# Three instead of two of eight gate and up tiles with seven products, and four low parts per block by a negative copy and an accumulating DMA

## The chip, the cores and the metric

The kernel runs on one core of a Trainium2 chip. The time is device microseconds of one launch. The engines are named as the profile names them: PE is TensorE (PEld its weight loads), ACT ScalarE, DVE Vector, POOL GpSimd, SP the engine that issues most DMAs.

## What is computed

One layer of an encoder trunk on 256 rows of 2048 float32 numbers: an input projection, three mixers, an output projection, then a SwiGLU block and a last norm. There is one layer; `w_gate` and `w_up` are 2048 by 5632. The change is in the two products `h @ w_gate` and `h @ w_up`.

```python
def rmsnorm(x, g):
    xf = x.astype(jnp.float32)
    y = xf * lax.rsqrt(jnp.mean(xf * xf, axis=-1, keepdims=True) + NORM_EPS)
    return (y * g.astype(jnp.float32)).astype(x.dtype)

def reference(x, positions, attn_norm_g, w_in, hg_lower_bounds, hg_norm_g, sb_norm_g,
              mla_q_norm_g, mla_w_uq, mla_kv_norm_g, mla_w_ukv, mla_out_norm_g, w_o,
              ffn_norm_g, w_gate, w_up, w_down, final_norm_g):
    ...
    for layer in range(DEPTH):
        h = rmsnorm(x, attn_norm_g[layer])
        hq, hf, hi, hg, sq, sk, sv, c_q, c_kv_rope = jnp.split(h @ w_in[layer], split_at, axis=-1)
        ...
        x = x + jnp.concatenate([hg_out, sb_out, mla_out], axis=-1) @ w_o[layer]
        h = rmsnorm(x, ffn_norm_g[layer])
        x = x + (jax.nn.silu(h @ w_gate[layer]) * (h @ w_up[layer])) @ w_down[layer]
    return rmsnorm(x, final_norm_g)
```

## The kernel before

**Matmuls in two halves.** A float32 operand is split into a high part in float32r and a low part, the rest: `hi = copy(raw)` on ScalarE, `lo = raw - hi` on Vector (L93, called by `split_w` at L107 and `halve` at L866). A product is then three matmuls: activation high times hi, activation high times lo, activation low times hi.

**The gate and up stage** (the loop over `g`, L933) has eleven blocks of 512 columns. In each, the inner dimension of 2048 is cut into eight tiles of 256. A plain tile loads one slab of w_gate and one of w_up, 512 KB each, as `raw` (L860), splits both, and `plain_unit` (L906) does 24 matmuls of 512 columns: two row halves (b) by gate and up by two inner halves (j) by three. They add into four accumulators c11, c21 (gate) and c12, c22 (up).

**The first two tiles (`FAST = 2`) are done with seven products instead of eight** (Strassen's scheme in Winograd's form, on a 2 by 2 grid of inner half by gate/up). `fast_weights` (L873) loads the up slab and the gate slab into one tile `W`, Vector makes four combinations `T`, and all operands are split (`hT`, `lT` for the combinations, `hi`, `lo` for those that are used as they are). The activations' eight forms are made once, in `turn_x2` (L812). The products fall into two groups: ACROSS (p1, p6, p7, p5) go into four PSUM banks and are shared by several outputs; ALONE (c11, c21, c12) go straight into accumulators. A fast tile has 7 x 3 = 21 matmuls. The loop first does ACROSS for all fast tiles, then ALONE for all, then sums the banks into u1 to u4 on Vector, then runs the plain tiles. At the block's end the accumulators are added, Silu is applied on ScalarE, and the result is turned by transposes in later blocks (`turn_hid`, L919, one step per plain tile by `tick`).

**Buffers.** raw, hi and lo have four slots each, `W`, `T`, `hT` and `lT` two each. A slot is written again when its last reader is done. The order on each engine is fixed when the program is built: a scheduler sorts by priority, and the loads and splits of weights stand 400 places ahead (`tc.high_priority(offset=ahead[0])`), so those of the next block are mixed into this one. Every engine's queue runs in order: an instruction that waits holds those behind it. SP issues the loads, in order too.

Of the kernel before, what the change touches and what calls it, by code (L numbers as in the profile page):

```python
# [9 lines left out]
F32 = mybir.dt.float32  # L10
F32R = mybir.dt.float32r
# [44 lines left out]
FAST = 2  # L56
# [4 lines left out]
def build(tc, x, xT, pos, gains, fgain, lbraw, w_in, w_uq, w_ukv, w_o, w_gate, w_up, w_down, cst, msk, out, dbg=None):  # L61
# [740 lines left out]
    def wo_end(a, g):  # L802
# [9 lines left out]
        def turn_x2():  # L812
            yield
            for i in range(2):
# [9 lines left out]
                A = ffp.tile([P, 8, P], F32, name=nm("T"), tag="T")  # L824
# [47 lines left out]

    def fast_weights(wa, wb, r0, c0):  # L873

        with tc.high_priority(offset=ahead[0]):
            W = ffp.tile([P, 4, 512], F32, name=nm("W"), tag="W")
            for w, js in ((wb, slice(0, 2)), (wa, slice(2, 4))):
                at = ROWS[w.tensor.name] * c0 + r0 * 512
                sp.dma_start(W[:, js, :], w[at:at + 2 * P * 512].rearrange("(p t c) -> p t c", p=P, t=2))
            T = ffp.tile([P, 4, 512], F32, name=nm("T"), tag="T")  # L880
            tt(T[:, 0:2, :], W[:, 0:1, :].broadcast_to([P, 2, 512]), W[:, 1:3, :], ALU.subtract)
            tt(T[:, 2, :], W[:, 1, :], T[:, 1, :], ALU.subtract)
            tt(T[:, 3, :], W[:, 3, :], T[:, 2, :], ALU.subtract)
            hT = ffp.tile([P, 4, 512], F32R, name=nm("hT"), tag="hT")
            lT = ffp.tile([P, 4, 512], F32R, name=nm("lT"), tag="lT")
            a = halve(W[:, 2:4, :], slice(0, 2))
            halve(T, slice(0, 2), hT, lT)
            halve(T, slice(2, 4), hT, lT)
            b = halve(W[:, 0:2, :], slice(1, 2))
        return a, b, (hT, lT)  # L890


    ACROSS = (("p1", 0, 0, 0), ("p6", 5, 2, 2), ("p7", 6, 2, 0), ("p5", 4, 2, 1))
    ALONE = (("c11", 2, 0, 1), ("c21", 3, 2, 3), ("c12", 7, 1, 1))

    def fast_unit(accs, products, ws, forms, start):
        ah, al = forms
        for name, f, which, k in products:
            hi, lo = ws[which]
            o = accs[name]  # L900
            last = name[0] == "p" and start == "last"
            pe.matmul(o, lhsT=ah[:, f, :], rhs=hi[:, k, :], start=start is True, stop=False)  # L902
            pe.matmul(o, lhsT=ah[:, f, :], rhs=lo[:, k, :], start=False, stop=False)  # L903
            pe.matmul(o, lhsT=al[:, f, :], rhs=hi[:, k, :], start=False, stop=last)  # L904
# [200 lines left out]
```

## Time and profile before

| | us |
|---|---|
| three runs | 1128.09, 1128.75, 1130.96 |
| median | 1128.75 |
| the profiled execution | 1129.1 |
| its span, first to last instruction | 1127.4 |
| one block of the gate and up stage in it | 43.3 |

The page gives busy time by engine and a mean over the whole run; stages differ, so the gate and up stage (about 400 to 877 us of the span) is read by itself, from the table of stretches and the timelines. A matmul's record is longer than its share of time, since matmuls overlap: the distance from start to start counts. The same holds, by less, for ScalarE and Vector.

### The profile page before, as it was taken

How to read it: one execution, taken by the hardware profiler on the slowest of the kernel's cores; microseconds unless marked ns; L12 is line 12 of the kernel's file. 1: busy time of each engine (PE TensorE's matmuls, PEld its weight loads, DVE VectorE, ACT ScalarE, POOL GpSimd, SP SyncE). 2: the span in 40 equal slices, each digit the busy share in tenths (PEclk: the TensorE clock that was granted, in tenths of full speed). 3: DMA queues.
4: the chain of work that ended last, by engine and by line, in shares of the span. 5: the costliest groups of instructions: out<-in, count | busy, mean ns of one | idle time of the engine just before them, and what ended most of it. 6: DMA issues, size and time to landing. Idle time of an engine off the chain costs nothing.

```text
span 1127.4 us, 14328 instructions
## 1 busy us (share of the span) xinstructions
PE 1112.2 (99%) x5363; PEld 942.3 (84%) x5363; DVE 758.9 (67%) x907; ACT 595.6 (53%) x793; POOL 77.4 (7%) x112
## 2 busy tenths in 40 slices
PE   8999999999999999999999999999999999999997
PEld 4888899999988888888888888888888888888886
DVE  7798555556557786786886887876967645454543
ACT  7664566566546654553554554554546534343433
POOL 3197000011100000000000000000000000000000
PEclk9999999999999999999999999999999999999999
DMA  7745455544776665655655656656638665666662
GB/s 259 245 152 164 123 170 179 168 134 157 217 250 203 218 214 187 204 191 189 201 191 184 207 185 204 197 171 209 198 119 291 205 197 188 194 195 189 189 198 99
DMA packets 73302, 215.18 MB, mean 191 GB/s; under 512 B 7440, under 2 KB 24592, under 8 KB 73232
## 3 DMA queue, kind: packets, MB, share of 16 engines
q1 hardware_dynamic: 72656, 212.16, 58.9%
q10 hardware_dynamic: 576, 2.10, 0.5%
q8 instruction: 42, 0.69, 0.2%
q14 instruction: 28, 0.23, 0.1%
HBM read 210.04 MB, written 4.19 MB: 190 GB/s over the span
## 4 chain that ended last, share of the span: by engine, by line
PE 95%; issue 1%; DVE 1%; ACT 1%; DMA 1%; POOL 0%; SPq 0%; ACTq 0%; POOLq 0%; DVEq 0%
PE acc L154 15%; PE acc L155 15%; PE acc L153 15%; PE acc L913 11%; PE acc L914 11%; PE acc L912 11%; PE bank L248 2%; PE bank L902 2%; PE bank L903 2%; PE bank L904 2%; PE acc L902 1%; PE acc L903 1%; PE acc L904 1%; DVE lo L93 1%; PE bank L411 1%
## 5 line engine op out<-in xcount | busy, mean ns | idle before, releaser
L93 DVE TENSOR_TENSOR lo<-raw,hi 128x1024 fp32r<-128x1024 f32 (+3 forms) x366 | 424.5, 1168 | 276.5 <-ACT hi L121 215.6
L121 ACT CAST hi<-raw 128x1024 fp32r<-128x1024 f32 (+3 forms) x234 | 223.1, 957 | 243.6 <-PE acc L155 220.7
L153 PE MATMUL acc<-hi,at 128*128 128x512 f32 (+2 forms) x808 | 304.8, 379 | 0.8 <-ACT hi L121 0.8
L154 PE MATMUL acc<-lo,at 128*128 128x512 f32 (+2 forms) x808 | 302.5, 375 | 3.0 <-DVE lo L93 2.8
L155 PE MATMUL acc<-hi,at 128*128 128x512 f32 (+2 forms) x808 | 301.4, 373 | 0.0
L912 PE MATMUL acc<-hi,at 128*128 128x512 f32 x528 | 207.5, 393 | 0.0
L914 PE MATMUL acc<-hi,at 128*128 128x512 f32 x528 | 205.8, 390 | 0.0
L913 PE MATMUL acc<-lo,at 128*128 128x512 f32 x528 | 205.7, 390 | 0.0
L869 ACT CAST hi<-raw 128x1024 fp32r<-128x1024 f32 x132 | 136.7, 1052 | 129.9 <-PE acc L914 95.8
L154 PEld LDWEIGHTS acc<-lo,at 128*128 128x128 f32 x808 | 152.1, 188 | 29.0 <-DVE lo L93 7.2
L153 PEld LDWEIGHTS acc<-hi,at 128*128 128x128 f32 x808 | 151.9, 188 | 23.9 <-ACT hi L121 1.9
L155 PEld LDWEIGHTS acc<-hi,at 128*128 128x128 f32 x808 | 151.9, 188 | 21.9
L913 PEld LDWEIGHTS acc<-lo,at 128*128 128x128 f32 x528 | 99.2, 188 | 20.6 <-DVE lo L93 0.7
L914 PEld LDWEIGHTS acc<-hi,at 128*128 128x128 f32 x528 | 99.1, 188 | 20.7
L912 PEld LDWEIGHTS acc<-hi,at 128*128 128x128 f32 x528 | 99.2, 188 | 19.8
L177 POOL TENSOR_TENSOR sm<-sm,expo 128x4 f32<-128x4 f32 (+2 forms) x14 | 12.0, 857 | 895.7 <-DVE sm L102 895.7
L93 DVE TENSOR_TENSOR lo<-W,hi 128x1024 fp32r<-128x1024 f32 (+1 forms) x44 | 42.0, 957 | 34.6 <-ACT hi L869 34.6
L869 ACT CAST hi<-W 128x1024 fp32r<-128x1024 f32 (+1 forms) x44 | 36.7, 834 | 49.8 <-PE acc L914 42.7
L93 DVE TENSOR_TENSOR lT<-T,hT 128x1024 fp32r<-128x1024 f32 x44 | 52.7, 1218 | 0.0
L869 ACT CAST hT<-T 128x1024 fp32r<-128x1024 f32 x44 | 45.2, 1049 | 0.3 <-DVE T L93 0.2
L93 DVE TENSOR_TENSOR T<-W,T 128x512 f32<-128x512 f32 x44 | 30.1, 684 | 0.1
L93 DVE TENSOR_TENSOR T<-W 128x1024 f32<-128x1024 f32 x22 | 26.9, 1221 | 1.4 <-DMA W<-w_gate 1.1
(254 smaller groups left out, 1097.4 us busy)
## 6 DMA issues: line engine op xcount, KB each, us to landing
raw<-w_down SPq DMA_DIRECT2D x88, 512.0 KB, 3.5
raw<-w_gate SPq DMA_DIRECT2D x66, 512.0 KB, 4.1
raw<-w_up SPq DMA_DIRECT2D x66, 512.0 KB, 4.4
raw<-w_in SPq DMA_DIRECT2D x48, 384.0 KB, 3.6
raw<-w_in SPq DMA_DIRECT2D x32, 512.0 KB, 3.6
raw<-w_o SPq DMA_DIRECT2D x32, 512.0 KB, 3.9
W<-w_up SPq DMA_DIRECT2D x22, 512.0 KB, 3.7
W<-w_gate SPq DMA_DIRECT2D x22, 512.0 KB, 4.6
```

The costliest lines, as they stand in the source:

```text
L93: dve.tensor_tensor(o, a, b, op=op)
L121: act.copy(hi[:, js, :n], raw[:, js, :n])
L153: pe.matmul(o, lhsT=ah, rhs=hi[:, j, cs], start=start and j == 0, stop=False)
L154: pe.matmul(o, lhsT=ah, rhs=lo[:, j, cs], start=False, stop=False)
L155: pe.matmul(o, lhsT=al, rhs=hi[:, j, cs], start=False, stop=stop and j == 1)
L869: act.copy(hi[:, js, :], src[:, js, :])
L902: pe.matmul(o, lhsT=ah[:, f, :], rhs=hi[:, k, :], start=start is True, stop=False)
L903: pe.matmul(o, lhsT=ah[:, f, :], rhs=lo[:, k, :], start=False, stop=False)
L904: pe.matmul(o, lhsT=al[:, f, :], rhs=hi[:, k, :], start=False, stop=last)
L912: pe.matmul(o, lhsT=ah, rhs=hi[:, j, :], start=start and nme == "c22" and j == 0, stop=False)
L913: pe.matmul(o, lhsT=ah, rhs=lo[:, j, :], start=False, stop=False)
L914: pe.matmul(o, lhsT=al, rhs=hi[:, j, :], start=False, stop=stop and j == 1)
```

## The change

`FAST` becomes 3, so each block has three fast and five plain tiles. In tiles 4 to 7 (`BYDMA`) the low part of the up slab is no longer subtracted on Vector: ScalarE writes `hi = copy(raw)` and then `lo = -hi`, and a DMA issued from POOL adds `raw` to `lo` in place (`halve_by_dma`). The four combinations are laid out anew: three in `T`, the fourth overwrites the first quarter of `W` (the up slab's first half, which is not needed any more); the gate slab comes as two DMAs of 256 KB. `hT`/`lT` hold what ACROSS needs (three combinations and one slab half as it is), and `alone_weights` splits what ALONE needs later. The products run as ACROSS of tiles 0 and 1, ALONE of 0, ACROSS of 2, ALONE of 1, ALONE of 2. `W` has three slots now, `T` one; the activations' forms (`A`) and four of the later stage's tiles move to other tags.

```diff
--- before.py
+++ after.py
@@ -53,7 +53,8 @@
 SABBUFS = 3
 WARM = 9
 RAWS = 4
-FAST = 2
+FAST = 3
+BYDMA = (4, 5, 6, 7)
 MAGIC = 12582912.0
 LOGEXP = "natural_log_exp_and_others"
 
@@ -821,7 +822,7 @@
                     x2T[n] = at
                     continue
 
-                A = ffp.tile([P, 8, P], F32, name=nm("T"), tag="T")
+                A = ffp.tile([P, 8, P], F32, name=nm("T"), tag="T", bufs=1)
                 for j in range(2):
                     act.activation(A[:, 2 * j:2 * j + 2, :], ps[:, j * 256:(j + 1) * 256].rearrange("p (b n) -> p b n", b=2),
                                    AF.Copy, scale=gc(G_FFN, 2 * n + j))
@@ -870,38 +871,54 @@
         tt(lo[:, js, :], src[:, js, :], hi[:, js, :].bitcast(F32), ALU.subtract)
         return hi, lo
 
+    def halve_by_dma(src):
+
+        hi = slabp.tile([P, 2, 512], F32R, name=nm("hi"), tag="hi")
+        lo = slabp.tile([P, 2, 512], F32R, name=nm("lo"), tag="lo")
+        act.copy(hi, src)
+        act.activation(lo, hi.bitcast(F32), AF.Copy, scale=-1.0)
+        pool.dma_start(lo, src, accum_op=ALU.add)
+        return hi, lo
+
     def fast_weights(wa, wb, r0, c0):
 
         with tc.high_priority(offset=ahead[0]):
-            W = ffp.tile([P, 4, 512], F32, name=nm("W"), tag="W")
-            for w, js in ((wb, slice(0, 2)), (wa, slice(2, 4))):
-                at = ROWS[w.tensor.name] * c0 + r0 * 512
-                sp.dma_start(W[:, js, :], w[at:at + 2 * P * 512].rearrange("(p t c) -> p t c", p=P, t=2))
-            T = ffp.tile([P, 4, 512], F32, name=nm("T"), tag="T")
-            tt(T[:, 0:2, :], W[:, 0:1, :].broadcast_to([P, 2, 512]), W[:, 1:3, :], ALU.subtract)
+            W = ffp.tile([P, 4, 512], F32, name=nm("W"), tag="W", bufs=3)
+            at = ROWS[wa.tensor.name] * c0 + r0 * 512
+            va, vb = (w[at:at + 2 * P * 512].rearrange("(p t c) -> p t c", p=P, t=2) for w in (wa, wb))
+            sp.dma_start(W[:, 0:2, :], vb)
+            sp.dma_start(W[:, 3, :], va[:, 0, :])
+            sp.dma_start(W[:, 2, :], va[:, 1, :])
+            T = ffp.tile([P, 3, 512], F32, name=nm("T"), tag="T", bufs=1)
+            tt(T[:, 0:2, :], W[:, 0:1, :].broadcast_to([P, 2, 512]), W[:, 1:4:2, :], ALU.subtract)
             tt(T[:, 2, :], W[:, 1, :], T[:, 1, :], ALU.subtract)
-            tt(T[:, 3, :], W[:, 3, :], T[:, 2, :], ALU.subtract)
-            hT = ffp.tile([P, 4, 512], F32R, name=nm("hT"), tag="hT")
-            lT = ffp.tile([P, 4, 512], F32R, name=nm("lT"), tag="lT")
-            a = halve(W[:, 2:4, :], slice(0, 2))
-            halve(T, slice(0, 2), hT, lT)
-            halve(T, slice(2, 4), hT, lT)
-            b = halve(W[:, 0:2, :], slice(1, 2))
-        return a, b, (hT, lT)
-
-
-    ACROSS = (("p1", 0, 0, 0), ("p6", 5, 2, 2), ("p7", 6, 2, 0), ("p5", 4, 2, 1))
-    ALONE = (("c11", 2, 0, 1), ("c21", 3, 2, 3), ("c12", 7, 1, 1))
-
-    def fast_unit(accs, products, ws, forms, start):
+            tt(W[:, 0, :], W[:, 2, :], T[:, 2, :], ALU.subtract)
+            hT, lT = wide("hT"), wide("lT")
+            split(hT[:, 0:3, :], lT[:, 0:3, :], T)
+            split(hT[:, 3, :], lT[:, 3, :], W[:, 3, :])
+        return W, (hT, lT)
+
+    def wide(tag):
+        return ffp.tile([P, 4, 512], F32R, name=nm(tag), tag=tag)
+
+    def split(hi, lo, src):
+        act.copy(hi, src)
+        tt(lo, src, hi.bitcast(F32), ALU.subtract)
+
+    def alone_weights(W):
+        with tc.high_priority(offset=ahead[0]):
+            h1, l1 = halve(W[:, 0:2, :], slice(0, 2))
+            h2, l2 = halve(W[:, 2:4, :], slice(0, 1))
+        return [(h1[:, 0, :], l1[:, 0, :]), (h1[:, 1, :], l1[:, 1, :]), (h2[:, 0, :], l2[:, 0, :])]
+
+
+    ACROSS = {"p1": (0, 3), "p6": (5, 2), "p7": (6, 0), "p5": (4, 1)}
+    ALONE = {"c11": (2, 2), "c21": (3, 0), "c12": (7, 1)}
+
+    def product(o, forms, f, hi, lo, start, stop):
         ah, al = forms
-        for name, f, which, k in products:
-            hi, lo = ws[which]
-            o = accs[name]
-            last = name[0] == "p" and start == "last"
-            pe.matmul(o, lhsT=ah[:, f, :], rhs=hi[:, k, :], start=start is True, stop=False)
-            pe.matmul(o, lhsT=ah[:, f, :], rhs=lo[:, k, :], start=False, stop=False)
-            pe.matmul(o, lhsT=al[:, f, :], rhs=hi[:, k, :], start=False, stop=last)
+        for lhsT, rhs, k in ((ah, hi, 0), (ah, lo, 1), (al, hi, 2)):
+            pe.matmul(o, lhsT=lhsT[:, f, :], rhs=rhs, start=start and k == 0, stop=stop and k == 2)
 
     def plain_unit(accs, wa, wb, at, start, stop):
         for nme, b, (hi, lo) in (("c11", 0, wa), ("c21", 1, wa), ("c12", 0, wb), ("c22", 1, wb)):
@@ -935,12 +952,26 @@
         fast = [fast_weights(w_gate, w_up, i * 256, g * 512) for i in range(FAST)]
         for n in ("p1", "p6", "p7", "p5"):
             accs[n] = bank()
-        for i in range(FAST):
-            fast_unit(accs, ACROSS, fast[i], x2T[i], True if i == 0 else "last" if i == FAST - 1 else False)
+
+        def across(i):
+            hT, lT = fast[i][1]
+            for n, (f, k) in ACROSS.items():
+                product(accs[n], x2T[i], f, hT[:, k, :], lT[:, k, :], i == 0, i == FAST - 1)
+
+        def alone(i):
+            ws = alone_weights(fast[i][0])
+            for n, (f, k) in ALONE.items():
+                product(accs[n], x2T[i], f, *ws[k], i == 0, False)
+
+        across(0)
+        across(1)
         for n in ("c11", "c21", "c12", "c22"):
             accs[n] = acc1()
-        for i in range(FAST):
-            fast_unit(accs, ALONE, fast[i], x2T[i], i == 0)
+        alone(0)
+        for i in range(2, FAST):
+            across(i)
+            alone(i - 1)
+        alone(FAST - 1)
         u1, u3, u2, u4 = part("s1"), part("u3"), part("u2", 2), part("v", 2)
         act.copy(u1, accs["p1"])
         tt(u2, u1, accs["p6"], ALU.add)
@@ -950,7 +981,8 @@
         for i in range(FAST, 8):
             with tc.high_priority(offset=ahead[0]):
                 wa = halve(load(w_gate, i * 256, g * 512), slice(0, 2))
-                wb = halve(load(w_up, i * 256, g * 512), slice(0, 2))
+                raw = load(w_up, i * 256, g * 512)
+                wb = halve_by_dma(raw) if i in BYDMA else halve(raw, slice(0, 2))
             plain_unit(accs, wa, wb, x2T[i], i == FAST, i == 7)
             if g == 0 and i == FAST:
                 flush()
@@ -970,7 +1002,7 @@
             at = act_tile()
         else:
             if n % 2 == 0:
-                pairs.append(ffp.tile([P, 2, 2, 2, 256], F32R, name=nm("T"), tag="T"))
+                pairs.append(ffp.tile([P, 2, 2, 2, 256], F32R, name=nm("W"), tag="W", bufs=3))
             at = pairs[-1][:, n % 2]
         f = hidf[n].rearrange("p (j n) -> p j n", j=2)
         act.copy(at[:, 0, :, :], f)
```

**Vector, from the last fast tile to the first plain tile.** Before (u, v and s are the block ends' parts, sm the row scale):

```order
L93 TENSOR_TENSOR lo_5602<-W_5584,hi_5601 128x512
L93 TENSOR_TENSOR T_5904<-W_5901 128x1024
L96 SCALAR_TENSOR_TENSOR u_1070_5319<-u_1070_5319,sm_3864,s_1068_5317 128x512
L93 TENSOR_TENSOR T_5904<-W_5901,T_5904 128x512
L96 SCALAR_TENSOR_TENSOR v_5320<-v_5320,sm_3864,u_1069_5318 128x512
L93 TENSOR_TENSOR T_5904<-W_5901,T_5904 128x512
L93 TENSOR_TENSOR u_1137_5657<-s_1135_5655,bank_5606 128x512
L93 TENSOR_TENSOR u_1136_5656<-u_1137_5657,bank_5607 128x512
L93 TENSOR_TENSOR T_5925<-W_5922 128x1024
L93 TENSOR_TENSOR lo_5667<-raw_5664,hi_5666 128x1024
L93 TENSOR_TENSOR T_5925<-W_5922,T_5925 128x512
L93 TENSOR_TENSOR lo_5673<-raw_5670,hi_5672 128x1024
```

Now:

```order
L94 TENSOR_TENSOR lT_6373<-T_6368,hT_6372 128x1536
L94 TENSOR_TENSOR lT_6373<-W_6364,hT_6372 128x512
L94 TENSOR_TENSOR T_6691<-W_6687 128x1024
L94 TENSOR_TENSOR lo_6457<-W_6364,hi_6456 128x1024
L94 TENSOR_TENSOR lo_6461<-W_6364,hi_6460 128x512
L94 TENSOR_TENSOR T_6691<-W_6687,T_6691 128x512
L94 TENSOR_TENSOR lT_6696<-W_6687,hT_6695 128x512
L94 TENSOR_TENSOR W_6687<-W_6687,T_6691 128x512
L94 TENSOR_TENSOR u_1295_6475<-s_1293_6473,bank_6379 128x512
L94 TENSOR_TENSOR lT_6696<-T_6691,hT_6695 128x1536
L94 TENSOR_TENSOR lo_6485<-raw_6482,hi_6484 128x1024
```

Behind the last fast tile's splits from `W` the next block's first tile now has all of its work (T, lT, W, lT) ahead of the first `lo<-raw`, where one 1024-wide T stood.

**ScalarE, around the plain tiles 5 and 6.** Before:

```order
L869 CAST hi_5751<-raw_5749 128x1024
L869 CAST hT_5929<-T_5925 128x1024
L869 CAST hi_5757<-raw_5755 128x1024
L928 COPY at_5700<-bank_5701 128x512
L869 CAST hi_5787<-raw_5785 128x1024
L869 CAST hi_5793<-raw_5791 128x1024
L928 COPY at_5700<-bank_5743 128x512
L869 CAST hi_5823<-raw_5821 128x1024
L869 CAST hi_5829<-raw_5827 128x1024
```

Now:

```order
L870 CAST hi_6570<-raw_6568 128x1024
L905 CAST hT_6709<-T_6705 128x1536
L878 CAST hi_6576<-raw_6574 128x1024
L945 COPY R_6518<-bank_6519 128x512
L879 ACTIVATE lo_6577<-hi_6576 128x1024
L870 CAST hi_6607<-raw_6605 128x1024
L878 CAST hi_6613<-raw_6611 128x1024
L945 COPY R_6518<-bank_6562 128x512
L879 ACTIVATE lo_6614<-hi_6613 128x1024
```

The up slab's `hi` is now followed by `lo<-hi`, the negative copy; the DMA `lo<-raw` on POOL waits for it.

**SP's loads of plain tiles, with what each waits for** (DMASW are the semaphores of POOL's DMAs, DMAHW those of SP's). Before:

```order
L863 DMA raw_5785<-w_gate 128x1024 [waits DMAHW1_49,DVE_49]
L863 DMA raw_5791<-w_up 128x1024 [waits DMAHW2_49,DVE_49]
L863 DMA raw_5821<-w_gate 128x1024 [waits DMAHW7_49,DMAHW3_49,DVE_49]
L863 DMA raw_5827<-w_up 128x1024 [waits DMAHW4_49,DMAHW0_49,DVE_49]
L863 DMA raw_5857<-w_gate 128x1024 [waits DMAHW5_49,DMAHW1_49,DVE_49]
L863 DMA raw_5863<-w_up 128x1024 [waits DMAHW6_49,DMAHW2_49,DVE_49]
```

Now, tiles 5 to 7 and the next block's first plain tile:

```order
L864 DMA raw_6568<-w_gate 128x1024 [waits DMAHW6_49,DVE_49]
L864 DMA raw_6574<-w_up 128x1024 [waits DMAHW7_49,DVE_49]
L864 DMA raw_6605<-w_gate 128x1024 [waits DMAHW0_49,DVE_49]
L864 DMA raw_6611<-w_up 128x1024 [waits DMAHW1_49,DMASW4_49,Activation_49]
L864 DMA raw_6642<-w_gate 128x1024 [waits DMAHW6_49,DMAHW2_49,DVE_49]
L864 DMA raw_6648<-w_up 128x1024 [waits DMAHW3_49,DMAHW0_49,DVE_49]
L864 DMA raw_6833<-w_gate 128x1024 [waits DMAHW7_49,DMAHW4_49,DMASW5_49]
```

The up slab of tile 6 now waits for a DMA of POOL, that of tile 4, which still reads the slot; before, each waited for Vector.

## Rows read from the trace of the kernel before

**Rows 1.** The page, whole run: busy us per engine; TensorE's granted clock.

```profile
PE 1112.2 (99%) x5363; PEld 942.3 (84%) x5363; DVE 758.9 (67%) x907; ACT 595.6 (53%) x793; POOL 77.4 (7%) x112
...
PEclk9999999999999999999999999999999999999999
```

**Rows 2.** Busy time by stretch: two blocks of the gate and up stage.

```profile
core 0: us, PE busy (x) PEld busy (x) DVE busy (x) ACT busy (x) POOL busy (x), PEclk, DMA share, GB/s
487.40:530.70 43.30, 43.30 (x195) 35.71 (x194) 33.48 (x37) 22.23 (x25) 0.00 (x0) 1.00 0.60 194
530.70:574.00 43.30, 43.30 (x196) 35.72 (x195) 33.43 (x37) 22.25 (x25) 0.00 (x0) 1.00 0.60 195
```

**Rows 3.** The page's chain by engine; waits: us, times, longest.

```profile
PE 95%; issue 1%; DVE 1%; ACT 1%; DMA 1%; POOL 0%; SPq 0%; ACTq 0%; POOLq 0%; DVEq 0%
...
PEld acc L154 <- DVE lo L93: 7.2, 11, 1.3
```

**Rows 4.** Timeline of TensorE, one block's start: start, us, instruction.

```profile
520.50 0.39 PE L912 MATMUL acc<-hi,at 128*128 128x512 f32 x1
...
530.48 0.39 PE L914 MATMUL acc<-hi,at 128*128 128x512 f32 x1
...
531.38 0.40 PE L902 MATMUL bank<-hT,at 128*128 128x512 f32 x1
...
533.48 0.40 PE L902 MATMUL bank<-hi,at 128*128 128x512 f32 x1
...
540.41 0.39 PE L912 MATMUL acc<-hi,at 128*128 128x512 f32 x1
540.63 0.39 PE L913 MATMUL acc<-lo,at 128*128 128x512 f32 x1
```

**Rows 5.** Line L902's instructions: duration min/median/max, first and last start.

```profile
L902 PE MATMUL bank<-hi,at x22: 389/392/396, 400.7 to 836.7; 128*128 128x512 f32 x22
```

**Rows 6.** Timeline of Vector, the same block's start.

```profile
531.06 0.68 DVE L93 TENSOR_TENSOR v<-v,acc 128x512 f32<-128x512 f32 x1
531.66 0.68 DVE L93 TENSOR_TENSOR lo<-W,hi 128x512 fp32r<-128x512 f32 x1
532.26 1.22 DVE L93 TENSOR_TENSOR T<-W 128x1024 f32<-128x1024 f32 x1
...
537.31 1.22 DVE L93 TENSOR_TENSOR T<-W 128x1024 f32<-128x1024 f32 x1
538.45 1.22 DVE L93 TENSOR_TENSOR lo<-raw,hi 128x1024 fp32r<-128x1024 f32 x1
...
540.19 3.49 DVE L93 TENSOR_TENSOR lo<-raw,hi 128x1024 fp32r<-128x1024 f32 x3
```

**Rows 7.** Timeline of ScalarE, the same block.

```profile
538.11 1.05 ACT L869 CAST hT<-T 128x1024 fp32r<-128x1024 f32 x1
539.06 2.95 ACT L869 CAST hi<-raw 128x1024 fp32r<-128x1024 f32 x3
...
547.05 0.58 ACT L928 COPY at<-bank 128x512 f32<-128x512 f32 x1
```

**Rows 8.** DMA: landing of all raw slabs; issues by tile, KB, us to landing.

```profile
DMA to landing us min/median/max: 2.8/3.7/6.8
...
raw<-w_up SPq DMA_DIRECT2D x66, 512.0 KB, 4.4
...
kept<-R ACTq DMA_DIRECT2D x4, 512.0 KB, 3.9
```

## The prediction

> **What bounds the kernel now.** I read the page's busy shares first: TensorE is busy 99% of the span at full granted clock, Vector 67%, ScalarE 53% [rows 1]. Then the stage table for two blocks of the gate and up stage: 43.30 us each, TensorE busy in all of it, Vector 33.5, ScalarE 22.2, DMA engines 0.60 at 194 GB/s [rows 2]. Then the waits and the chain: the chain is 95% TensorE, and what TensorE waits for Vector in the whole run is a few us [rows 3]. So in this stage time is the number of matmuls times their spacing, as long as every hi and lo lands in time. The stage starts at 400.7; the second tile's p1 in the last block starts at 836.7, 2.8 us into that block, so a block takes (836.7 - 2.8 - 400.7) / 10 = 43.3 us, eleven times [rows 5].
>
> Spacing: 44 matmuls lie between 520.50 and 530.48, so 0.2268 us each, though one shows 0.39 (they overlap). Those that stream hT or lT are wider apart: nine from 531.38 to 533.48, 0.2333 each [rows 4].
>
> **Part 1, the third fast tile.** A fast tile has 21 matmuls, a plain one 24; a block goes from 186 to 183. That removes 3 x 0.2268 = 0.680 us. Four of a fast tile's seven products read hT and lT, before and now, so twelve more matmuls per block take the wider spacing: 12 x 0.0065 = 0.078 back. Net 0.602 us per block, 6.6 us in eleven. The transposes stay, and nothing outside the stage changes in number. The loads carry the same bytes (a fast tile's gate slab is two DMAs); each costs SP 0.33 us of queue, and SP idles between loads.
>
> **Part 2, Vector.** From row to row a 1024-wide TENSOR_TENSOR takes 1.14 us (three in 3.49) and a 512-wide 0.60 [rows 6]; a 1536-wide one is new, and I put it on the same line, 1.67. A fast tile costs 1.14 + 0.60 + 0.60 for the forms and 1.67 + 0.60 + 1.14 + 0.60 for the low parts, 6.35, as it did. The third one replaces two plain splits (2.28), and four more splits (4.56) go away: 6.35 - 6.84 = -0.5 us of 33.5 per block. No room is won, but none is lost.
>
> Where Vector is tight is the turn of the block. Before, it had the first plain slab's lo done at 538.45 + 1.22 = 539.67, and TensorE wanted it at 540.63: 0.96 us to spare [rows 4, 6]. Now the third tile's hT slot comes free only after the first tile's four products, F + 2.97 (F is the block's start; 12 x 0.2333, the last one ends 0.40 after it starts). ScalarE writes the 1536-wide hi until F + 4.52, and from there Vector's order runs without a gap: lT 1.67, lT 0.60, T 1.14, lo 1.14, lo 0.60, T 0.60, lT 0.60, W 0.60, u 0.60, lT 1.67, then the first plain lo 1.22. That is 10.4, done at F + 15.0. TensorE wants it after 36 matmuls at 0.2333, 27 at 0.2268 and three hi products of the plain tile: F + 15.2. Margin 0.2: I take nothing, and if a duration is off, ten blocks pay it (the last has no next tile queued in front).
>
> **Part 3, the accumulating DMA.** ScalarE gains four 1024-wide passes per block at 0.95 from start to start [rows 7], 3.8, and about 1.4 for the tile: 22.2 becomes some 27.4 of 43; its cover stays. POOL is idle in this stage [rows 2]; its queue now holds 44 DMAs, and the small POOL instruction for r2 stands behind the first one, half a block ahead of its first reader. DMA engines: at 194 GB/s for a share of 0.60 they move 323 GB/s when busy, so 512 KB is 1.62 us of all sixteen; four per block at one to two passes add 0.15 to 0.30 to the share.
>
> What counts is x, the time from POOL's release to the landing of the sum. The up slab of unit i gets its hi slot when unit i - 2 has ended. Then ScalarE does hi (0.95 to the next start), a copy of a transposed part (0.58, so 0.48) and the negative copy (1.05 to its end) [rows 7], so POOL is released 2.5 to 3.2 us after that. TensorE reads the slab's lo at 2.95 us into unit i; a unit is 24 x 0.2268 = 5.44, plus 0.44 where transposes follow. That leaves x 6.1 us for tiles 4, 6 and 7, and 5.6 for tile 5, whose hi waits behind the next block's 1536-wide hT. There is a second path: tile 6's up slab is loaded into the raw slot that tile 4's accumulation holds (SP waits for it, and two loads stand behind it). Vector's T is done at F + 10.4; behind it ScalarE's queue holds hT 1.42, four hi at 0.95, hT 0.48 and the negative copy 1.05, so POOL is released for tile 4 at F + 17.2. Then come x, a load of 3.7 to 4.4 [rows 8], 2.5 on ScalarE, and x again, against F + 34.7 (F + 14.5, three units, two turns of 0.44, and 2.95). So 2x is at most 10.5 to 11.2. I take the limit at 5.4 us. Beyond it two accumulations in series pay: 2 us per block for each us of x, 22 us in the run.
>
> The price of x is in no row: no accumulating DMA, none from POOL, none from SBUF to SBUF. Nearest rows: a raw slab lands 2.8 us after issue at least, 3.7 in the middle, 6.8 at most; the SBUF to DRAM copy takes 3.9 [rows 8]. The sum must read its destination too, which I put at a second pass, 1.62. Below: 2.8, if that read hides. Above: 6.8 + 1.62 = 8.4. I take 3.7 + 1.62 = 5.3, nearest to the common slab: just within 5.4. At the ends the run takes 1122.5, and 1122.5 + 22 x 3.0 = 1188.5.
>
> The Trainium skill ("DMA: Bandwidth & Descriptors", section "Anatomy of one DMA — SWDGE (gpsimd) path") fits a DMA from GpSimd by 2.0 us plus bytes over 436e3 per us; for 512 KB that is an estimate of 3.2 us, with no word on accumulation. By it x has 2 us to spare, the time is 1122.5, and the first two rivals below fall. No row here shows such a DMA, and the loads in the trace land later than that, so I give it no weight.
>
> **Sum.** The profiled execution took 1129.1 us (span 1127.4, 1.7 around it), 0.35 above the median of 1128.75. 1129.1 - 6.6 = 1122.5.
>
> **The rivals.**
> *Late sums (slower).* x is over 5.4 because the destination is read at a slower rate, or because loads run beside it at a share of 0.60. TensorE then waits for lo in plain units, at L930. For: four slabs in a row are treated so, each within half a us of its limit. Against: the chosen x already has a full second pass in it. At x = 6.5: 1122.5 + 22 x 1.1 = 1146.7. The total passes 1132.5 from x = 5.85 on.
> *Vector holds up POOL's descriptors (slower).* While the accumulations are issued (F + 17 to F + 34), Vector runs up to 1.67 us at a time. If POOL can't write them until the instruction ends, x is 5.3 + 1.67 = 7.0, and the run 1122.5 + 22 x 1.6 = 1157.7. The trace has no POOL work here to show it. The Trainium skill ("SBUF — State Buffer", section "Who interferes with whom") says that Vector shuts GpSimd out in its two-port modes, that TENSOR_TENSOR has none, and that with two SBUF inputs it contends only with GpSimd instructions that read SBUF: by that rule this rival falls, and no run here shows it yet.
> *Vector's turn of the block (no change).* The margin of 0.2 is not there, say 0.5 us are missing at the first plain lo in ten blocks: 1122.5 + 5 = 1127.5. For it: before, 0.96 was spare at that place and 10.4 us in a row now lead to it. Against: the rest of the stage gives Vector 10 us of idle time per block.
>
> **How the numbers follow.** All lands in time: 0.50, 1121 to 1126. Late sums: 0.33, mostly 1124 to 1170. Descriptors held: 0.09. Vector's turn: 0.08. The predicted time is that of the first, 1122.5. About 0.3% is what a measurement of this kernel can tell from no change: 1125.7 to 1132.5 is no change. Faster: 0.48 (nearly all of the first case). No change: 0.11 (Vector's turn, and bits of its neighbours). Slower: 0.41. The range runs from 1121, where all 7.5 us of the 33 matmuls are kept, to 1163, which is x = 7.2; above it lie some 0.07 of the late sums and half of the held descriptors. The range of the first case alone is 1121 to 1126.
>
> **What would show it.** Right: 5330 instead of 5363 matmuls; blocks of 42.7 us; no idle time of TensorE at L930 behind the DMA of lo; POOL's lo<-raw landing in 5.4 us or less; DMA share 0.75 to 0.90. Wrong: blocks over 43.3 with TensorE waiting for lo from DMA (late sums; the landing time says how late, and whether it is longest where Vector is busiest), or waiting for lo from Vector in the first plain tile (the turn). Wrong in another way: a granted clock below full, if TensorE gets idle gaps, or loads that land so much later beside the accumulations that ScalarE waits for raw.

## The result, and the profile of the changed kernel

| | before | after |
|---|---|---|
| median of five runs, us | 1128.62 | 1189.69 |
| lowest and highest | 1127.78, 1130.96 | 1185.85, 1193.05 |
| span of the profiled execution | 1127.4 | 1190.2 |
| ratio, 95% interval | | 1.0538 [1.0517, 1.0559] |

The changed kernel is 61 us slower. The forecast was 1122.5 and the range 1121 to 1163, so both the sign and the range were wrong. *Late sums*, a rival with 0.33, is what happened, and by more than its own range.

The page of the changed kernel, first. Beside [rows 1] and [rows 3] it shows busy time by engine, the granted clock, the chain by engine, and the costliest groups (busy, mean ns | idle time before, releaser):

```profile
PE 1125.6 (95%) x5330; PEld 942.7 (79%) x5330; DVE 752.8 (63%) x921; ACT 654.9 (55%) x860; POOL 115.0 (10%) x156
...
PE 72%; DMA 17%; issue 6%; ACT 2%; DVE 2%; SPq 0%; POOLq 0%; ACTq 0%; POOL 0%; DVEq 0%
...
L930 PE MATMUL acc<-lo,at 128*128 128x512 f32 x440 | 179.9, 409 | 50.0 <-DMA lo<-raw 49.9
...
L878 ACT CAST hi<-raw 128x1024 fp32r<-128x1024 f32 x44 | 46.3, 1053 | 79.8 <-DMA raw<-w_up 68.5
...
raw<-w_gate SPq DMA_DIRECT2D x55, 512.0 KB, 6.0
raw<-w_up SPq DMA_DIRECT2D x55, 512.0 KB, 5.3
lo<-raw POOLq DMA_DIRECT2D x44, 512.0 KB, 6.9
```

The 33 matmuls are gone (5330), yet TensorE is busy 13.4 us longer and idle 49.4 us longer (1190.2 - 1125.6 = 64.6, before 1127.4 - 1112.2 = 15.2). The idle time has one place: L930, the products with lo in plain tiles, waiting for the accumulation: 22.5 us at tile 4, 24.5 at tile 6, 2.9 at tile 7, none at tile 5. The chain, 95% TensorE before, has 17% DMA in it. The accumulation lands in 6.9 us in the middle, and the loads are later than before too, w_up 5.3 for 4.4 [rows 8].

Two blocks by stretch, as in [rows 2] (columns as there):

```profile
497.00:546.90 49.90, 44.98 (x192) 36.11 (x191) 32.73 (x38) 27.55 (x31) 3.46 (x4) 0.97 0.75 213
595.10:643.30 48.20, 43.24 (x192) 34.93 (x191) 32.45 (x37) 27.63 (x31) 3.48 (x4) 1.00 0.75 218
```

A block takes 47 to 51 us for 43.3 (these two 49.9 and 48.2). ScalarE's 27.6 and the DMA share of 0.75 are as forecast, and Vector's load is light: by their means none of the three is full.

The chain of the second of these blocks, in order of time (start, us, what):

```profile
612.76 8.07 DMA lo<-raw
620.84 0.02 SPq L864
620.86 0.05 issue
620.91 6.38 DMA raw<-w_up
...
627.35 2.89 issue
630.25 0.01 POOLq L880
630.26 4.96 DMA lo<-raw
635.22 0.04 issue
635.26 0.50 PE acc L930
```

This is the second path of the prediction, link by link. Tile 4's sum takes 8.07 us; only then does SP issue tile 6's load into the slot that it held; the load takes 6.38, ScalarE's part about 2.9, tile 6's sum 4.96. TensorE idled 2.24 us at tile 4 (at 620.88) and 2.72 at tile 6 (at 635.26).

SP's issues just ahead of the sums in that block (start, us):

```profile
610.04 0.33 SPq L864 DMA_DIRECT2D raw<-w_gate  x1
611.17 0.33 SPq L864 DMA_DIRECT2D raw<-w_up  x1
612.31 0.33 SPq L864 DMA_DIRECT2D raw<-w_gate  x1
...
624.97 0.33 SPq L864 DMA_DIRECT2D raw<-w_gate  x1
632.08 0.33 SPq L864 DMA_DIRECT2D raw<-w_up  x1
```

Tile 4's sum starts at 612.76 with three loads issued in the 2.7 us before it, and takes 8.1. Tile 5's (619.13) and tile 6's (630.26) have none in the 5 us before them, and take 5.8 and 5.0. Tile 7's (633.24) has one 1.2 us before it and takes 7.4.

The rest, TensorE's longer busy time, is for the most part clock. Stretches around two such waits of another block (PE busy is the second number, PEclk the third from the end):

```profile
520.00:525.00 5.00, 2.68 (x12) 1.90 (x11) 5.00 (x8) 1.75 (x2) 0.86 (x1) 1.00 0.85 156
525.00:530.00 5.00, 5.00 (x26) 4.13 (x25) 0.53 (x1) 0.72 (x1) 0.00 (x0) 1.00 0.95 324
...
535.00:538.50 3.50, 1.29 (x5) 1.05 (x6) 1.23 (x1) 0.68 (x1) 0.88 (x1) 0.99 0.99 236
538.60:541.80 3.20, 3.20 (x9) 2.52 (x8) 0.00 (x0) 0.50 (x1) 0.00 (x0) 0.50 0.99 245
542.00:545.00 3.00, 3.00 (x15) 2.48 (x14) 1.95 (x3) 1.26 (x2) 0.00 (x0) 1.00 0.58 157
```

TensorE was busy 2.68 of 5.00 us, then, after a busy stretch, 1.29 of 3.50; behind that the granted clock is 0.50, the 1.2 GHz level, and nine matmuls take the time of fourteen. That happens in some blocks only: eight such stretches lie between 425 and 935 us, with 26.8 us of TensorE's busy time in them, so half of that, 13.4 us, is what the clock costs. Over 400 to 940 us the granted clock is 0.97.

A smaller part comes with each wait itself. The matmuls around the wait of 2.72 us:

```profile
632.15 0.39 PE L929 MATMUL acc<-hi,at 128*128 128x512 f32 x1
635.26 0.50 PE L930 MATMUL acc<-lo,at 128*128 128x512 f32 x1 [2.72 <-DMA lo<-raw]
635.60 0.40 PE L931 MATMUL acc<-hi,at 128*128 128x512 f32 x1
```

Two steps from start to start take 3.45 us here; at the usual spacing of 0.227 and with the wait they would take 3.17. So the overlap that is lost at a wait costs some 0.28 us more, at full clock, and is counted as busy time.

### The profile page after: what moved, and what is told of

The parts are those of the page before. It is cut to its first block, busy times and chain, and to the rows that moved or that the text cites. A ratio compares the mean times of both kernels' runs of the same rounds, so it can differ in the third digit from the quotient of the medians.

```text
span 1190.2 us, 14526 instructions
## 1 busy us (share of the span) xinstructions
PE 1125.6 (95%) x5330; PEld 942.7 (79%) x5330; DVE 752.8 (63%) x921; ACT 654.9 (55%) x860; POOL 115.0 (10%) x156
## 3 DMA queue, kind: packets, MB, share of 16 engines
q0 software_dynamic: 6336, 23.07, 11.2%
## 4 chain that ended last, share of the span: by engine, by line
PE 72%; DMA 17%; issue 6%; ACT 2%; DVE 2%; SPq 0%; POOLq 0%; ACTq 0%; POOL 0%; DVEq 0%
PE acc L155 15%; PE acc L156 15%; PE acc L154 15%; DMA lo<-raw 12%; PE bank L921 7%; PE acc L921 5%; DMA raw<-w_up 4%; PE acc L930 4%; PE acc L931 3%; PE acc L929 3%; PE bank L249 1%; DVE lo L94 1%; PE bank L412 1%; PE acc L591 0%; PE acc L590 0%
## 5 line engine op out<-in xcount | busy, mean ns | idle before, releaser
L94 DVE TENSOR_TENSOR lo<-raw,hi 128x1024 fp32r<-128x1024 f32 (+3 forms) x300 | 344.1, 1156 | 285.0 <-ACT hi L122 218.8
L930 PE MATMUL acc<-lo,at 128*128 128x512 f32 x440 | 179.9, 409 | 50.0 <-DMA lo<-raw 49.9
L931 PE MATMUL acc<-hi,at 128*128 128x512 f32 x440 | 176.3, 401 | 0.0
L929 PE MATMUL acc<-hi,at 128*128 128x512 f32 x440 | 174.9, 405 | 0.0
L154 PEld LDWEIGHTS acc<-hi,at 128*128 128x128 f32 x808 | 151.8, 188 | 23.9 <-ACT hi L122 1.9
L156 PEld LDWEIGHTS acc<-hi,at 128*128 128x128 f32 x808 | 151.7, 188 | 22.1
L930 PEld LDWEIGHTS acc<-lo,at 128*128 128x128 f32 x440 | 85.7, 195 | 78.0 <-DMA lo<-raw 61.0
L94 DVE TENSOR_TENSOR lo<-W,hi 128x1024 fp32r<-128x1024 f32 x66 | 62.2, 957 | 65.7 <-ACT hi L870 65.7
L931 PEld LDWEIGHTS acc<-hi,at 128*128 128x128 f32 x440 | 85.9, 195 | 17.8
L929 PEld LDWEIGHTS acc<-hi,at 128*128 128x128 f32 x440 | 85.4, 194 | 18.1
L880 POOL DMA_DIRECT2D lo<-raw x44 | 38.4, 872 | 567.5 <-ACT lo L879 281.0
L870 ACT CAST hi<-W 128x1024 fp32r<-128x1024 f32 x66 | 55.0, 833 | 68.6 <-PE acc L931 58.1
L878 ACT CAST hi<-raw 128x1024 fp32r<-128x1024 f32 x44 | 46.3, 1053 | 79.8 <-DMA raw<-w_up 68.5
L921 PE MATMUL bank<-hT,at 128*128 128x512 f32 x264 | 86.6, 396 | 0.0
L870 ACT CAST hi<-raw 128x1024 fp32r<-128x1024 f32 x66 | 67.0, 1046 | 14.3 <-DMA raw<-w_gate 14.3
L94 DVE TENSOR_TENSOR lT<-T,hT 128x1536 fp32r<-128x1536 f32 x33 | 57.9, 1754 | 18.2 <-ACT hT L905 18.2
L905 ACT CAST hT<-T 128x1536 fp32r<-128x1536 f32 x33 | 48.9, 1481 | 34.6 <-PE bank L921 22.7
```

The costliest lines, as they stand in the source:

```text
L94: dve.tensor_tensor(o, a, b, op=op)
L154: pe.matmul(o, lhsT=ah, rhs=hi[:, j, cs], start=start and j == 0, stop=False)
L156: pe.matmul(o, lhsT=al, rhs=hi[:, j, cs], start=False, stop=stop and j == 1)
L870: act.copy(hi[:, js, :], src[:, js, :])
L878: act.copy(hi, src)
L905: act.copy(hi, src)
```

## Experiments

The theory after the result: an accumulation costs some 4.6 to 5 us by itself, plus the loads that lie ahead of it in the DMA engines; TensorE pays where that exceeds the limits of the prediction. The rivals: the accumulation is dear wherever it stands; POOL or Vector delays it; the new layout costs. Where no interval is given, the time is one execution.

### The parts alone

```diff
-BYDMA = (4, 5, 6, 7)
+BYDMA = ()
```

> All low parts by subtraction on Vector again (BYDMA empty), three fast tiles kept: the first part of the change alone. Theory (the whole loss is the accumulating DMA's): Vector has 33.0 + 4 x 1.14 = 37.6 of 42.7 us per block and still keeps up, blocks of 42.7 us, 1122.5 us, 1121 to 1126. Rival (the new layout itself costs: the order ACROSS, ALONE, the single T slot, Vector's turn of the block): blocks over 43.3, TensorE waits for lo or lT from DVE in the first plain tile, 1128 to 1150.

Measured: 1123.52 us, ratio 0.9951 [0.9935, 0.9968]. A block, and the page's row for L930:

```profile
487.10:529.80 42.70, 42.70 (x192) 35.13 (x191) 37.21 (x42) 24.02 (x27) 0.00 (x0) 1.00 0.62 196
```

```profile
L930 PE MATMUL acc<-lo,at 128*128 128x512 f32 x440 | 171.2, 389 | 0.0
```

The third fast tile gives 5.5 us, in blocks of 42.7, with Vector at 37.2 and no wait. So the layout is right and the turn of the block holds; the accumulations cost all of the rest. Against this kernel the changed one has 48.7 us more idle time of TensorE and 19.8 us more busy time for the same matmuls (1125.6 against 1105.8): 68.5, the difference of the spans. Of the 19.8, the low clock accounts for 13.4; the 6.4 left are 0.26 for each of the 25 waits.

```diff
-FAST = 3
+FAST = 2
```

> Two fast tiles as in the kernel before (in the new layout) with the four accumulations: the second part of the change alone. Theory (the loss belongs to the accumulations and hangs on the same limits): 1129 plus about 66, 1180 to 1200, lo<-raw at tile 4's place in about 8 us. Rival (it needs the third fast tile beside it, as in its turn of the block): 1130 to 1150.

Measured: 1166.4, between the two expectations. That is some 38 us over the kernel before (the new layout with two fast tiles and no accumulation was not run), so the loss does not need the third fast tile. But with two fast tiles the loads fall elsewhere: tile 4's sum takes 4.8 us in the middle and TensorE never waits there, tiles 5 to 7 wait 5.0, 13.8 and 7.7 us, and the median landing is 6.2 us.

### Which place, how many

```diff
-BYDMA = (4, 5, 6, 7)
+BYDMA = (4,)      # and (6,), and (5, 7)
```

> One accumulation per block, in tile 4; tiles 5 to 7 subtract on Vector. Theory (x is about 4.9 us alone plus the loads that lie ahead of it in the DMA engines; 8.1 us at tile 4's place against a direct limit of 6.1): lo<-raw still lands in 7 to 8.5 us there, TensorE idles about 2 us at L930 in each block and then runs some matmuls at the lower clock, 2.5 to 3 us per block over the 42.7 of the kernel without such DMAs: 1150 to 1158. Rival (accumulations delay one another and the loads, so that one alone is harmless): lands in 5 to 6 us, 1123 to 1127.

> One accumulation per block, in tile 6. In the changed kernel it is issued with hardly any load in the DMA engines and lands in 5.0 us, but its raw slab comes late behind tile 4's accumulation, which is gone here. Theory (queue of loads decides): 5 to 6 us if the place is as quiet as before, no idle time at L930, 1123 to 1126. Rival (any accumulation costs a wait, 6 to 8 us wherever it stands): 1140 to 1158.

> Accumulations in tiles 5 and 7 alone. Tile 5's lands in 5.5 us in the changed kernel, against a limit of 5.6; tile 7's in 7.2 against 6.1, with 1 MB of loads in its time. Theory (x is 4.9 plus what lies ahead): tile 5 idles 0 to 0.5 us, tile 7 about 1 us where its loads lie as before: 1124 to 1140. Rival (place does not matter): both idle 2 us and the clock falls, 1160 to 1175.

Measured: tile 4 alone 1150.6, tile 6 alone 1122.6, tiles 5 and 7 1126.9. Min, median and max of the landing, of tile 4 alone and then of tile 6 alone:

```profile
DMA to landing us min/median/max: 5.9/7.8/8.0
```

```profile
DMA to landing us min/median/max: 4.5/4.6/5.3
```

The same instruction with the same bytes takes 7.8 us at one place and costs 27 us; at the other it takes 4.6 and costs nothing. Tile 4 alone leaves TensorE idle 18.9 us at L930, 1.7 in each block. Landing less wait is 5.9 us in the middle of the blocks: that is the direct limit, for the prediction's 6.1. The DMA share doesn't tell the two apart. Over 430 to 860 us it is 0.61 in the bad case and 0.64 in the harmless one:

```profile
430.00:860.00 430.00, 411.35 (x1812) 334.90 (x1811) 341.55 (x382) 238.18 (x267) 7.85 (x9) 0.99 0.61 194
```

```profile
430.00:860.00 430.00, 429.93 (x1923) 353.36 (x1923) 364.76 (x412) 257.42 (x298) 9.50 (x11) 1.00 0.64 205
```

For tiles 5 and 7 the landings were 4.7 in the middle and 6.9 at most, 3.2 us of idle time in the run; tile 7 was quieter than expected, as without the other two accumulations its median landing was 5.3 us for 7.2.

### Loads ahead of one accumulation

Tile 6's alone, the harmless one, with one or two loads beside it:

```diff
         act.activation(lo, hi.bitcast(F32), AF.Copy, scale=-1.0)
+        beside = ffp.tile([P, 2, 512], F32, name=nm("beside"), tag="beside", bufs=1)
+        act.copy(beside[:, 0, 0:1], lo[:, 0, 0:1].bitcast(F32))
+        act.dma_start(beside, w_down[0:2 * P * 512].rearrange("(p t c) -> p t c", p=P, t=2))
         pool.dma_start(lo, src, accum_op=ALU.add)
```

> The kernel with tile 6's accumulation alone, which lands in 4.6 us and costs nothing, and beside it one more load of 512 KB into a tile that nobody reads, issued from ScalarE's queue behind the negative copy, so within half a us of POOL's issue (POOL's release comes one one-column copy later). Theory (x is 4.6 plus the loads that lie ahead in the DMA engines): 512 KB at the 323 GB/s of before is 1.6 us, so the sum lands in 5.6 to 6.6, about at the limit of 6.1: 1122.5 to 1128. Rival (the landings of 7 to 9 us came of something else than loads in front: of tile 4's place, of several accumulations): 4.6 to 5.0 us, 1122 to 1124.

> As with one load, with two of 512 KB beside tile 6's accumulation. Theory: 7.0 to 8.4 us, as at tile 4's place in the changed kernel, where 1.1 MB of other packets lie in the same time; 1 to 2 us over the limit of 6.1 in each block and some matmuls at the lower clock: 1136 to 1152. Rival: under 5.5 us, 1122 to 1125.

Measured: 1147.1 and 1190.7 us, against 1122.6 with none. The line of the DMA (its waiters in us and times, and its landing), one load and then two:

```profile
  PE acc L933: 18.6, 11
...
DMA to landing us min/median/max: 6.9/7.3/7.8
```

```profile
  PE acc L934: 44.7, 11
...
DMA to landing us min/median/max: 8.9/9.3/10.8
```

None, one, two loads: 4.6, 7.3, 9.3 us. A load of 512 KB in front costs the accumulation 2.0 to 2.7 us, more than the 1.6 that I had worked out. This settles the cause of the long landings: no place, no other accumulation and no slot differs between the three (the one-column copies of 0.19 us only start POOL 0.2 to 0.3 us later). The price in time is steeper than expected as well (1122.5 to 1128 and 1136 to 1152 were): with two loads TensorE idles 4.1 us in each block and is busy 23.4 us longer (1128.7 against 1105.3) for the same matmuls, at a granted clock of 0.95 over the same stretch:

```profile
430.00:860.00 430.00, 394.39 (x1675) 320.01 (x1674) 318.66 (x356) 223.16 (x267) 8.11 (x9) 0.95 0.65 204
```

### Fewer loads, no addition, a busier Vector

```diff
-                wa = halve(load(w_gate, i * 256, g * 512), slice(0, 2))
                 raw = load(w_up, i * 256, g * 512)
+                wa = halve(raw if i in BYDMA else load(w_gate, i * 256, g * 512), slice(0, 2))
```

> In tiles 4 to 7 the gate slab is not loaded; the up slab is split once more in its place (the gate columns of these tiles are left out), so that ScalarE, Vector, TensorE and POOL do the same work and the stage loads 2 MB per block less, of 8. Theory (the loads beside it make the accumulation long): lo<-raw lands in 4.0 to 5.5 us instead of 6.9. Rival (the accumulation itself costs that much): 6.3 to 7.0. In both the raw slots are easier, so the time itself falls: about 1122 to 1130 at x under 5.6, 1140 to 1160 at x near 7.

Measured: 1147.8; the sum lands in 4.5, 5.5, 8.8 us (min, median, max), and tile 4, whose sum now takes 5.4, idles no more. The landing agrees with the theory; the time is above what it gave for a median of 5.5. The late ones pay: TensorE's idle time at L930 is 14.3 us, in tiles 5 to 7 of some blocks (2.8, 4.3 and 6.8 us), where sums still take up to 8.8. At tile 4, where the changed kernel is late first, the last load in front is now 1.6 us ahead of the sum instead of 0.4 (in the blocks around 506 and 612 us), and the sum goes from 8.1 to 5.4 us.

```diff
-        pool.dma_start(lo, src, accum_op=ALU.add)
+        pool.dma_start(lo, src)
```

> POOL's DMA copies raw over lo instead of adding it, so the low part of these four slabs is not the right one (that part of the computation is left out); issue, bytes written, waits and order stay. Theory (reading the destination and adding is what makes x long): lo<-raw lands in 3.5 to 5.0 us in the middle instead of 6.9, and the run takes 1122 to 1140. Rival (the transfers beside it make x long): lands in 5.5 to 6.9, 1160 to 1190. Second rival (POOL's issue or Vector's port): lands within 0.3 us of the sum's 6.9, 1185 to 1195.

Measured: 1151.8, landing 3.5, 6.0, 8.5. The time lies between the two expectations, the landing in the range of the first rival. So both the addition and the company count. The same 44 DMAs as sums, then as copies (packets, MB, share of 16 engines):

```profile
q0 software_dynamic: 6336, 23.07, 11.2%
```

```profile
q0 software_dynamic: 6336, 23.07, 5.5%
```

The sum holds the DMA engines twice as long as a copy (11.2% of 1190.2 us is 133, 5.5% of 1150.0 is 63). The copy alone would still have cost some 28 us over the kernel without any.

```diff
                 wb = halve_by_dma(raw) if i in BYDMA else halve(raw, slice(0, 2))
+                if i in BYDMA:
+                    again = ffp.tile([P, 2, 512], F32, name=nm("again"), tag="again", bufs=1)
+                    tt(again, x2T[6].bitcast(F32), x2T[7].bitcast(F32), ALU.subtract)
```

> The changed kernel with one more 1024-wide subtraction on Vector in each of tiles 4 to 7, of two resident tiles into one that nobody reads: 4.6 us per block, 37.6 in all, no transfer and no wait added. Theory (Vector has no part in x): lo<-raw lands in 6.9 us in the middle as before, POOL's own 0.87 us stays, 1185 to 1195. Rival (Vector holds up the descriptors or the reading of SBUF): POOL's own time or the landing grows by 0.3 us or more in the middle, 1197 or more.

Measured: 1197.2. The time fell on the rival's side, the landing did not: 4.5, 5.9, 8.8 us, POOL's own time 0.87 as before, and TensorE waits less for the sum (40.6 us against 49.9). Its span is 5.2 us longer: TensorE's busy time grew by 4.6, for as many matmuls (the mean granted clock of the run is 0.981 for 0.987), and a new wait (6.1 us, once, at L249 for ScalarE's `s`) stands against the shorter ones. No sign that Vector has a part in x.

### The limits

```diff
-RAWS = 4
+RAWS = 5
```

> Five raw slots instead of four; nothing else. Tile 4's accumulation now holds back the gate slab of tile 7 and no longer the up slab of tile 6. Theory (the path accumulation, raw slot, next load, next accumulation costs most): SP's wait for lo<-raw ahead of a load of w_up and ScalarE's 68.5 us of waits for raw<-w_up mostly go; what stays is x of about 7 against a direct limit of 5.6 to 6.1, twice in series, 2 to 3 us per block: 1145 to 1160. Rival (the direct wait is all): 1180 to 1195, TensorE's idle time at L930 stays at 50 us.

In `plain_unit`, the products with hi first and those with lo last (with four slots, and with five):

```diff
                 pe.matmul(o, lhsT=ah, rhs=hi[:, j, :], start=start and nme == "c22" and j == 0, stop=False)
-                pe.matmul(o, lhsT=ah, rhs=lo[:, j, :], start=False, stop=False)
-                pe.matmul(o, lhsT=al, rhs=hi[:, j, :], start=False, stop=stop and j == 1)
+                pe.matmul(o, lhsT=al, rhs=hi[:, j, :], start=False, stop=False)
+        for nme, b, (hi, lo) in (("c11", 0, wa), ("c21", 1, wa), ("c12", 0, wb), ("c22", 1, wb)):
+            for j in range(2):
+                ah = at[:, 0, j, b * P:(b + 1) * P]
+                pe.matmul(accs[nme], lhsT=ah, rhs=lo[:, j, :], start=False, stop=stop and j == 1)
```

> The order of products with lo last, but four raw slots as in the changed kernel. Theory (tile 4 is late by the direct limit alone, tile 6 by the path through the raw slot): the reordering alone lifts the direct limit to about 9 us, so tile 4 idles 0 to 1 us as with five slots; tile 6 gains 1.6 us of the 2.3 by its later reading and more by the earlier tile 4: 0 to 1.5 us. Blocks of 43.7 to 45.5, 1134 to 1153. Rival (the fifth slot did it): tile 6 idles over 2 us, 1160 or more.

> All four accumulations, five raw slots, and in plain_unit the products with hi first and those with lo last: the up slab's lo is read 4.5 us into a unit instead of 2.95, and its hi slot comes free 1.8 us sooner. Nothing in the accumulation gets cheaper. Theory (a direct limit of 6.1 and a slot path are overrun by 2 us each): the limit becomes about 9 us, TensorE's idle time at L930 falls from 50 us to under 10, full clock, 1122.5 to 1132. Rival (the DMA engines as such are short of time, or what is lost is not the wait for lo): idle time moves to other lines, 1160 to 1195.

Measured: five slots alone 1191.8, lo last alone 1161.7, both 1143.1. Five slots alone were a miss. They do remove the path through the slot: tile 6 idles no more and ScalarE waits for w_up no more. But tile 4's sum still has its loads in front and takes 8.4 us in the middle, the waits at tile 4 and tile 7 grow to 28.8 and 12.6 us (22.5 and 2.9 in the changed kernel), and TensorE waits 41.4 us in all and is busy 4.0 us longer. With lo last and four slots, 9 us above the upper end of its expectation, tile 4 idles half a us a block, tile 6 1.3, and the path through the slot remains:

```profile
ACT hi L878 <- DMA raw<-w_up: 66.1, 19, 7.7
```

With both it is 8.1 us in the run, and TensorE's wait is down to 10.4 us, although the landings are no shorter (median 7.7). So most of the loss was the wait for lo at two limits: lo last takes back 28 us by itself, the fifth slot nothing by itself and 19 us more with it. The kernel with both still misses its expectation (1132 at most) and takes 20 us more than the one without accumulations; 10.4 of them are waits at tiles 4 and 7 and 6.0 longer busy time, and the rest is not settled.

### A version that beats both

```diff
-FAST = 3
-BYDMA = (4, 5, 6, 7)
+FAST = 4
+BYDMA = (6,)      # and (5, 7), and ()
```

> Four fast tiles, and tile 6's up slab alone by the accumulating DMA, which idled nothing with three. It removes three more matmuls per block, net 6 to 6.6 us as the third fast tile did (5.5 measured): 1116.5 to 1117.5. Vector goes to 37.6 + 4.1 - 1.1 = 40.6 of 42.1 us per block. Rival (Vector is now too full, or the slots of W are too few for four tiles): TensorE waits for lT or lo from DVE, 1125 to 1160.

> Four fast tiles with accumulations in tiles 5 and 7, the pair that idled 3 us in the whole run with three fast tiles. Vector goes to 39.5 us per block, one subtraction less than with tile 6 alone. Theory (what the kernel with four fast tiles and tile 6 lacks to 1117 is Vector's room): 1117 to 1121. Rival (two accumulations with loads ahead of them now cost more than Vector's 1.1 us): 1123 to 1135.

> Four fast tiles and no accumulating DMA: Vector has 41.7 us of work in a block of 42.1. Theory (Vector is then too full, and one accumulation is what makes the fourth fast tile possible): TensorE waits for lT or lo from DVE, 1122 to 1135, slower than the 1120.7 with tile 6 by DMA. Rival (the accumulation gives nothing here either): 1117 to 1120.

Measured: tile 6 by DMA 1120.71, ratio 0.9930 [0.9912, 0.9949], so 0.7% faster than the kernel before; tiles 5 and 7 1163.13, 1.0299 [1.0266, 1.0333]; none 1130.63, 1.0014 [0.9999, 1.0030]. Nine blocks of the kernel with tile 6 by DMA, then of the one with none:

```profile
455.00:830.00 375.00, 374.47 (x1668) 305.86 (x1667) 355.15 (x402) 234.01 (x266) 7.85 (x9) 1.00 0.67 212
```

```profile
455.00:830.00 375.00, 371.43 (x1652) 301.97 (x1651) 361.55 (x404) 226.62 (x254) 0.00 (x0) 1.00 0.60 199
```

With four fast tiles and no DMA Vector is busy 361.55 of 375 us, and TensorE loses 3 us more than with one accumulation and does 16 matmuls fewer in the same time; it waits for Vector's `v` at the transposes. One quiet accumulation is worth 10 us between the medians here; the 16 matmuls of these nine blocks are 3.6 of them, and the profiled executions differ by 8, so part of it is not accounted for. Two were worse than both expectations. With four fast tiles more loads are under way at tile 5's place (in the block from 495 us on two slabs of 512 KB are issued in the 1.5 us before its sum, with three fast tiles the last one 2.6 us before it): the sum lands in 7.8 us there, and TensorE idles 32.6 us at L930. The best kernel misses my 1117 by 4 us; I have not settled where they are.

## Why the prediction was wrong

**Part 1, the third fast tile: right.** Net 6.6 us expected, 5.5 measured alone (the interval allows 3.6 to 7.3), 5330 matmuls, blocks of 42.7.

**Part 2, Vector and the turn of the block: right.** The first plain lo was done at F + 15.0 in the block above (F = 595.05), as forecast; the margin of 0.2 us was enough there and, with Vector fuller, in the kernel without accumulations. The rival named after it fell.

**Part 3, the path: right.** The chain above goes through the very links that were written down. POOL was released for tile 4 at 612.76, F + 17.7, for 17.2: the negative copy ended at F + 17.3, and POOL started 0.4 us later, as at the block's other tiles, which stood in no term. The direct limit was 5.9 at tile 4 for 6.1; the runs with added loads give 5.6 with POOL's start 0.2 to 0.3 us later. (The written terms give 5.9 without and 6.3 with transposes, and 10.6 to 11.3 for 2x; the differences of 0.1 to 0.2 decide nothing.) Summed up, the path ended at F + 40.2 for F + 34.7: 0.5 us from POOL's release, 2.8 from x at tile 4, 2.0 from the load (6.4 for 4.4), 0.5 from ScalarE's part with POOL's start, less 0.3 from x at tile 6. TensorE's two waits in that block are 5.0 us.

**Part 3, the price of x: the step that failed.** I took 5.3, the median landing of a load plus a second pass. That is about what a sum takes with few loads around it (4.6 to 5.0 in the middle). But x was then used as one number for four places, and at tile 4, where the path starts, it is 8.1 in the middle (6.5 to 8.5): there loads lie ahead, and each costs 2.0 to 2.7 us. The upper bound of 8.4 had about the right size, from a load's worst landing; the error was to treat it as a tail and not as what happens at that place in nearly every block. That the sum at this bound, 1188.5, comes near the measured 1189.69 is luck: x was 8.1 at one place of four, and 20 us of the loss are no wait.

The Trainium skill ("DMA: Bandwidth & Descriptors", section "Anatomy of one DMA — SWDGE (gpsimd) path") gave an estimate of 3.2 us for 512 KB. No sum here was that fast: 4.5 at least. The plain copy came near it, with 3.5 at its quickest and 6.0 in the middle. (That the loads of [rows 8] land later than 3.2 holds for their middle, 3.7, and not for the quickest, 2.8.)

**The load beside it: mis-sized.** 3.7 to 4.4 us in the path through the slot; it was 6.38 in the block above, issued 1.8 us behind tile 5's sum, with two more loads issued 0.4 and 2.0 us behind it.

**From x to the time: mis-sized.** 22 us of run per us of x beyond 5.4, with no term for the clock: at 6.9 this gives 1155. The measured loss has 20 us that are no wait: 13 from stretches at a granted clock of 0.50, and 6 from the overlap that is lost at each wait. The prediction named the first among what would prove it wrong and gave it no price. The added busy time isn't in proportion to the wait: with tile 4 alone 18.9 us of waits came with 6.1 us of it (1111.9 against 1105.8), with two loads beside tile 6 44.7 came with 23.4.

**Vector holds up POOL's descriptors: fell.** 4.6 us more of Vector's work per block left POOL's instruction at 0.87 us and the landing no longer. The Trainium skill ("SBUF — State Buffer", section "Who interferes with whom") says that TENSOR_TENSOR with two inputs in SBUF contends only with GpSimd's own reads of SBUF; the trace agrees, with POOL's 0.87 us unchanged.

## What to carry to other kernels

Price a DMA that stands in a tight loop by what is issued just ahead of it at that place, not by its own duration or the mean share of the DMA engines. Where several such steps lie in series, look for the place that the first limit starts from, and ask how late it is there. Put such a transfer where the queue is quiet, and only where the engine that it relieves is really the bound: here one of four was worth having, and only with a fourth fast tile (1120.7 us against 1130.6; with three 1122.6 against 1123.5).

## What the runs showed of the hardware

- An accumulating DMA of 512 KB from SBUF to SBUF, issued by POOL, lands in 4.5 us at best and 4.6 in the middle at a quiet place; with one and two loads of the same size issued just ahead of it, in 7.3 and 9.3. POOL itself is taken for 0.87 us, 0.53 for a plain copy.
- For the same bytes, 44 times 512 KB, it holds the DMA engines 133 us where a plain copy holds them 63 (11.2% and 5.5% of the runs).
- Waits of TensorE cost more than themselves. With 4.1 us of idle time in each block the granted clock of 430 to 860 us was 0.95, with 1.7 us in each block 0.99 (tile 4 alone) and 1.00 (one load beside tile 6). At full clock a wait costs some 0.3 us of lost overlap besides.
